# First expert gather taken apart, overflow loop in a branch, residual formed later: one change to a mixture-of-experts kernel

## The chip, the cores and the metric

One core of one Trainium2 chip runs the whole kernel as one program. The metric is device time in microseconds (us) of one execution, and the number before is the median of three runs. The profile comes from one further execution, whose own time is given beside its span. Engines are named as in the profile: PE (matrix products), PEld (weight loads of PE), DVE (vector), ACT (scalar), POOL (GpSimd), SP (sync, which here only issues loads). All the weights are float32 and are read from HBM once.

## The reference

One decoder layer over 256 tokens of width 2048. What matters here is the middle and the end of it: a router picks two of 16 experts for each token, and the experts' weights, 3 x 8 MB each, are by far most of the bytes.

```python
x = layer_norm(ALPHA * x + mix, ln1_g[i], ln1_b[i])
ffn = grouped_top2_moe(x, w_router, b_router, w_e_gate[i], w_e_up[i], w_e_down[i])
x = layer_norm(ALPHA * x + ffn, ln2_g[i], ln2_b[i])
x = x + jax.nn.sigmoid(x @ w_ple_gate[i]) * (p[i] @ w_ple_proj[i])

# grouped_top2_moe, for expert e and the rows xb that chose it
hid = jax.nn.silu(xb @ w_gate[e]) * (xb @ w_up[e])      # 2048 -> 1024, twice
y   = (hid @ w_down[e]) * src_w[:, None]                # 1024 -> 2048
```

## The kernel before

The program runs in stages, and each engine executes its instructions in the order in which the code writes them. The head (input projection, gated DeltaNet, pooling, output projection) ends with the first layer norm, whose standardised rows lie in `x1`, and with the router. Then come the 16 experts' gate and up products, expert by expert (the loop `for e in range(NE)`), then all down products, one chunk of output columns after the other (`CH`, five chunks of 512, 512, 512, 256 and 256 columns) with the last gate matrix between them, and a tail that normalises and writes.

**Pieces and slots.** Gate and up weights travel in pieces of 128 partitions x 1024 floats (4 KB per partition, 512 KB in all). Two neighbouring rows of a gate or up matrix lie as one run of 8 KB in HBM; a load of whole runs fills two pieces. A piece waits for its product in a slot: `ring` (5) and `ht` (3) hold two pieces each, `pre` (6) and `raw` (4) one piece each. That is 26 pieces. `begin` issues the next load into a free slot, on SP's queue; if a two-piece slot meets two halves of the same run it is one load of 8 KB runs, otherwise two loads of 4 KB runs. `freed` is called when PE has read a piece and starts the next load into that slot at once.

**Gather.** Experts are handled in pairs. A one-hot matrix `P` (DVE, L971) picks the rows of `x1` that chose the two experts, 64 places each. `gather` multiplies `P` by `x1` in four column blocks (L1000), brings each to SBUF (L1006), transposes it (L1012) and writes it to the tile `X` (L1019, or L1024 and L1026 for the first pair, where the norm's scale and bias are applied on the way). The first gather runs whole before the first product; the next one is run in steps between the products of the first expert of the pair before.

**Residual.** After the first gather DVE multiplies `x1` by the norm's scale and adds its bias in place (L1100, L1101), from four broadcast rows that ACT's queue had loaded, and ACT writes ALPHA times that to `r0` (L1102).

**Overflow.** If more than 64 tokens choose one expert, the rest goes through a loop with a trip count read from memory (`overflow`, L1114 to L1193). It stands before expert 2 (`OVER = 2`). In the profiled execution the count is zero. A loop is built from blocks: a jump that skips the body, a skip block in which each engine waits until its own work is done (for SP: all loads that it has issued), and an exit block in which each engine waits for all the others.

**Products.** A piece is used by two product instructions, one per expert half of the array (L1089), which the trace shows as four rows. `step()` and `estep()` advance the side jobs (evacuation, gather, hidden layer) by one step after each piece.

Of the kernel before, what the change touches and what calls it, by code (L numbers as in the profile page):

```python
# [10 lines left out]
F32 = mybir.dt.float32  # L11
# [10 lines left out]
NE = 16  # L22
# [8 lines left out]
RING, HTS, HLN, OVER = 5, 3, 8, 2  # L31
# [12 lines left out]
def trunk(tc, x, p, w_in, conv_w, a_log, dt_bias, dn_norm_w, pool_w, pool_scale, w_out,  # L44
# [4 lines left out]
    with es:  # L49
# [646 lines left out]
        SLOTS = {"ring": (RING, 2), "ht": (HTS, 2), "pre": (6, 1), "raw": (4, 1)}  # L696
# [6 lines left out]
        def slot_tile(tag, dtype=F32):  # L703
            bufs, n = SLOTS[tag]
            return spool[tag].tile([128, 1024 * n], dtype, name=tag, tag=tag, bufs=bufs)
# [91 lines left out]
        row4 = {}  # L797
# [31 lines left out]
        for cs, ks in wout_order[1:]:  # L829
            for c in cs:  # L830
# [13 lines left out]
        for tag in ("raw", "pre"):  # L844
            for _ in range(SLOTS[tag][0]):
                begin(tag)
# [77 lines left out]
        def choice():  # L924
# [5 lines left out]
            nc.vector.tensor_copy(ntoti, ntot)  # L930
            nc.vector.tensor_reduce(c2[1], pr, axis=AX.X, op=ALU.add)
# [25 lines left out]
        for _ in range(HTS):  # L957
            begin("ht")

# [32 lines left out]
        def gather(P, X, raw=False):  # L992
# [22 lines left out]
            def put(c, ps):  # L1015
                v = X[c // 2][:, c % 2 * 4:c % 2 * 4 + 4]
                ps = ps.rearrange("p (k s) -> p k s", s=128)
                if not raw:
                    (nc.vector.tensor_copy if c % 2 else nc.scalar.copy)(v, ps)  # L1019
                    return  # L1020
                for i in range(4):
                    g, b = (ln1p[:, i % 2, n, 2 * c + i // 2:2 * c + i // 2 + 1] for n in range(2))
                    if c % 2:
                        nc.vector.tensor_scalar(v[:, i], ps[:, i], g, b, op0=ALU.mult, op1=ALU.add)  # L1024
                    else:
                        nc.scalar.activation(v[:, i], ps[:, i], AF.Identity, bias=b, scale=g)  # L1026
# [87 lines left out]
        def overflow():  # L1114
            trips = nc.values_load(ntoti[0:1, 0:1], min_val=0, max_val=(2 * S - 1) // (SL + 1))
            with tc.For_i(0, trips, 1):  # L1116
# [30 lines left out]
                for c in range(2):  # L1147
                    ps = pt().rearrange("p (j s) -> p j s", s=SL)
                    for i in range(8):
                        d = c * 1024 + i // 2 * 256 + i % 2  # L1150
                        for t in range(NB):
                            nc.tensor.matmul(ps[:, i], x1[:, t, d:d + 256 - i % 2:2], Pv[:, t], start=(t == 0), stop=(t == NB - 1))
                    nc.scalar.copy(Xv[:, c * 8:c * 8 + 8], ps)
# [20 lines left out]
                nc.scalar.copy(Cv[SL:128], ps[0:SL, 0:S])  # L1174
                for c in range(4):
                    cs = slice(c * 512, (c + 1) * 512)
                    Y = pa()
                    for f0 in range(0, 8, 2):
                        src = wd[ds(e * DE + f0 * 128, 256), cs].rearrange("(k p) c -> p k c", p=128)
                        w = load(src, hl_tile("raw"))  # L1180
                        for i, v in enumerate(HALVES):
                            f = f0 + i
                            nc.tensor.matmul(Y[v], hv[0][:, f // 4, f % 4], w[:, i * 512:(i + 1) * 512], start=(f0 == 0), stop=(f0 == 6))
                    yy = hl_tile("yy", F32R).rearrange("p (n c) -> p n c", n=2)
                    nc.scalar.activation(yy[:, 0], Y, AF.Copy, scale=gv)
                    nc.vector.scalar_tensor_tensor(yy[:, 1], Y, gv, yy[:, 0], op0=ALU.mult, op1=ALU.subtract)
                    for t in range(NB):
# [3 lines left out]
                        nc.vector.tensor_add(r0[:, t, cs], r0[:, t, cs], ps)  # L1191
# [597 lines left out]
```

## Time and profile before

| what | value |
|---|---|
| median of 3 runs | 1578.21 us (1577.09 to 1580.15) |
| the profiled execution's own time | 1575.58 us |
| span of its instructions | 1573.7 us |
| PE busy | 1457.8 us, 93% of the span |
| DVE, ACT, POOL busy | 29%, 20%, 9% |
| bytes moved | 491.70 MB, mean 312 GB/s |

A stretch of the span is read in three steps: how busy the DMA engines are in it and how many GB/s they move, whether PE waits in it and for what, and what stands in the chain of work that ended last. A busy share of DMA of 1 or a little more means that the core's 16 DMA engines never pause.

### The profile page before, as it was taken

The numbers are of one execution on the slowest core, as the hardware profiler recorded it, in microseconds if no ns is written. First come the engines' busy times: TensorE is split into PE (matmuls) and PEld (weight loads), VectorE is DVE, ScalarE is ACT, GpSimd is POOL, SyncE is SP. The second block draws the span as 40 slices with busy tenths as digits, with TensorE's granted clock in tenths as the row PEclk, the third lists the DMA queues.
The fourth block names the chain that finished last, engine by engine and source line by source line (L and its number), as shares of the span: only waits on it lengthen the run. The fifth ranks groups of instructions, "written<-read, shape, count | busy, mean of one in ns | idle before, by whom it ended". The sixth has DMA issues, their size and how long they took to land.

```text
span 1573.7 us, 19926 instructions
## 1 busy us (share of the span) xinstructions
PE 1457.8 (93%) x8058; PEld 813.6 (52%) x8058; DVE 462.7 (29%) x866; ACT 313.5 (20%) x584; POOL 134.7 (9%) x210
## 2 busy tenths in 40 slices
PE   8999999999969759989889899988999999999997
PEld 8999989987833213322223232321233444546765
DVE  5885777665460000000001010000100101113335
ACT  4443443243331000000001010100010111002123
POOL 1251034310000000000000000000000000000023
PEclk9999999999999979999999999999999999999999
DMA  8544453448837969999999999999999999999991
GB/s 252 163 140 117 125 163 106 121 135 265 330 130 273 411 250 387 409 415 412 418 416 409 412 412 409 413 413 409 402 387 386 382 379 381 380 378 346 349 352 60
DMA packets 204387, 491.70 MB, mean 312 GB/s; under 512 B 18442, under 2 KB 64707, under 8 KB 193795
## 3 DMA queue, kind: packets, MB, share of 16 engines
q1 hardware_dynamic: 198784, 487.64, 83.8%
q10 hardware_dynamic: 5426, 2.48, 0.6%
q8 instruction: 65, 1.06, 0.3%
q14 instruction: 32, 0.25, 0.0%
q0 software_dynamic: 80, 0.26, 0.0%
HBM read 488.23 MB, written 2.10 MB: 312 GB/s over the span
## 4 chain that ended last, share of the span: by engine, by line
DMA 37%; PE 25%; DVE 1%; ACT 0%; issue 0%; POOL 0%; SPq 0%; ACTq 0%
PE pa L1640 9%; DMA ring<-in_w_e_up 7%; DMA ring<-in_w_e_gate 7%; DMA ht<-in_w_e_gate 5%; PE pa L1089 4%; PE pa L1558 4%; DMA ht<-in_w_e_up 4%; DMA ring<-in_w_e_down 3%; DMA ht<-in_w_e_down 3%; DMA pre<-in_w_e_gate 2%; DMA pre<-in_w_e_up 2%; PE pt L1000 2%; DMA ht<-in_w_ple_gate 2%; PE pt L1558 2%; PE pt L1456 2%; DMA pre<-in_w_e_down 1%
## 5 line engine op out<-in xcount | busy, mean ns | idle before, releaser
L1089 PE MATMUL pa<-ring,X 128*64 128x512 f32 x856 | 209.1, 606 | 21.2 <-DMA ring<-in_w_e_up 10.8
L658 PE MATMUL pp<-xh,hi 128*128 128x256 f32 x640 | 188.3, 294 | 0.0
L658 PE MATMUL pp<-xl,hi 128*128 128x256 f32 x640 | 179.7, 281 | 0.0
L658 PE MATMUL pp<-xh,lo 128*128 128x256 f32 x640 | 179.6, 281 | 0.0
L611 DVE TENSOR_TENSOR lo<-raw,hi 128x512 fp32r<-128x512 f32 x206 | 149.2, 748 | 90.3 <-ACT hi L610 90.0
L1089 PE MATMUL pa<-ht,X 128*64 128x512 f32 x648 | 159.3, 604 | 16.4 <-DMA ht<-in_w_e_gate 8.4
L610 ACT CAST hi<-raw 128x512 fp32r<-128x512 f32 x206 | 119.2, 618 | 140.1 <-PE pp L658 99.7
L1089 PE MATMUL pa<-pre,X 128*64 128x512 f32 x464 | 116.3, 607 | 30.7 <-SPq L1116 25.8
L1089 PEld LDWEIGHTS pa<-ring,X 128*64 128x64 f32 x856 | 52.8, 136 | 146.4 <-issue 66.9
L658 PEld LDWEIGHTS pp<-xh,hi 128*128 128x128 f32 x640 | 122.3, 191 | 0.2
L658 PEld LDWEIGHTS pp<-xl,hi 128*128 128x128 f32 x640 | 122.3, 191 | 0.1
L658 PEld LDWEIGHTS pp<-xh,lo 128*128 128x128 f32 x640 | 121.9, 190 | 0.1
L1078 DVE SCALAR_TENSOR_TENSOR evac<-evac,pt 128x512 f32<-128x512 f32 x16 | 11.0, 687 | 370.0 <-ACT evac L1075 370.0
L1089 PEld LDWEIGHTS pa<-ht,X 128*64 128x64 f32 x648 | 39.6, 136 | 113.2 <-issue 50.6
L1442 DVE SCALAR_TENSOR_TENSOR evac<-pa,gs,evac 128x512 fp32r<-128x512 f32 (+1 forms) x40 | 25.7, 642 | 190.0 <-ACT evac L1440 190.0
L1640 PE MATMUL pa<-ht,raw 128*64 128x512 f32 (+1 forms) x308 | 80.6, 511 | 0.7 <-DMA ht<-in_w_e_down 0.7
L1047 ACT COPY evac<-pa 128x512 f32<-128x512 f32 x32 | 18.8, 586 | 313.5 <-PE pa L1089 313.5
L1089 PEld LDWEIGHTS pa<-pre,X 128*64 128x64 f32 x464 | 28.7, 137 | 97.7 <-issue 61.3
L1640 PE MATMUL pa<-ring,pre 128*64 128x512 f32 (+1 forms) x296 | 78.0, 520 | 1.1 <-DMA ring<-in_w_e_down 1.1
L1000 PE MATMUL pt<-x,P 128*64 128x512 f32 x256 | 64.3, 627 | 12.6 <-DVE P L971 12.5
L1640 PE MATMUL pa<-ring,raw 128*64 128x512 f32 (+1 forms) x256 | 68.0, 514 | 1.1 <-DMA ring<-in_w_e_down 1.1
L1640 PE MATMUL pa<-ht,pre 128*64 128x512 f32 (+1 forms) x244 | 64.8, 517 | 1.0 <-DMA ht<-in_w_e_down 1.0
(377 smaller groups left out, 1807.0 us busy)
## 6 DMA issues: line engine op xcount, KB each, us to landing
ring<-in_w_e_down SPq DMA_DIRECT2D x111, 512.0 KB, 10.8
ht<-in_w_e_down SPq DMA_DIRECT2D x110, 512.0 KB, 10.5
raw<-in_w_in SPq DMA_DIRECT2D x80, 512.0 KB, 3.7
ring<-in_w_e_up SPq DMA_DIRECT2D x62, 512.0 KB, 10.2
pre<-in_w_e_gate SPq DMA_DIRECT2D x60, 512.0 KB, 10.2
ring<-in_w_e_gate SPq DMA_DIRECT2D x29, 1024.0 KB, 13.6
pre<-in_w_e_up SPq DMA_DIRECT2D x56, 512.0 KB, 10.2
ht<-in_w_e_gate SPq DMA_DIRECT2D x53, 512.0 KB, 10.2
```

The costliest lines, as they stand in the source:

```text
L610: nc.scalar.copy(hi[:, k], raw[:, k])
L611: nc.vector.tensor_sub(lo[:, k], raw[:, k], hi[:, k])
L658: nc.tensor.matmul(o, a[:, k, hc], b[:, kk], start=(first and n == 0), stop=(last and n == 2), skip_group_check=True)
L1000: nc.tensor.matmul(ps[v], P[:, t, a], x1[:, t, c * 512:(c + 1) * 512], start=(t == 0), stop=(t == NB - 1))
L1047: nc.scalar.copy(raw, acc)
L1078: nc.vector.scalar_tensor_tensor(h, h, 1.0, tr[0], op0=ALU.add, op1=ALU.mult)
L1089: nc.tensor.matmul(acc[v], X(kk), w[:, h * 512:(h + 1) * 512], start=(kk == 0), stop=(kk == KC - 1))
L1442: nc.vector.scalar_tensor_tensor(yy[1], Y, gs[:, e:e + 1], yy[0], op0=ALU.mult, op1=ALU.subtract)
L1456: nc.tensor.matmul(pR[c][t], C[:, e, t * 128:(t + 1) * 128], yy[n], start=(e == 0 and n == 0 and (t == 0 or w == 512)), stop=(e == NE // 2 ...
L1558: nc.tensor.matmul(ps[:, 0:S + 2], a[:, o:o + 128], b[:, k], start=(k == 0 and n == 0), stop=(k == kn - 1 and n == len(pairs) - 1))
L1640: nc.tensor.matmul(Y[v], HS[2 * e + a][:, f // 4, f % 4], two_[a][0][:, j * w:(j + 1) * w], start=(f == 0), stop=(f == 7))
```

## The change

It does six things. (1) The first gather is done without transposes: `gather0` multiplies a block of `x1` (as weights, with every second column) by `P` and gets `X` in its final layout; two of its four blocks run before the first product, the other two just before pieces 0 and 4 of expert 0. (2) Each later gather starts one expert later, with the second expert of the pair before. (3) `x1` is left standardised; every gather applies scale and bias on its way to `X`, and `r0` starts as zeros (POOL) and is filled by the new side job `residual`, from expert 1 on. The four broadcast rows are no longer loaded. (4) The overflow loop moves ahead of expert 0 and into a branch, `tc.If(trips > 0, ...)`. (5) `pre` has 8 slots instead of 6, the pool `hl` 6 tiles instead of 8, and two `X` tiles that are not yet needed are lent to the first loads ("X", `lent`). (6) Single slots are refilled two at a time, so that two-piece slots always meet whole 8 KB runs.

```diff
-RING, HTS, HLN, OVER = 5, 3, 8, 2
+RING, HTS, HLN = 5, 3, 6
...
-        SLOTS = {"ring": (RING, 2), "ht": (HTS, 2), "pre": (6, 1), "raw": (4, 1)}
+        SLOTS = {"ring": (RING, 2), "ht": (HTS, 2), "pre": (8, 1), "raw": (4, 1), "X": (4, 1)}
...
-                if c == 1:
-                    for n, v in (("g", ln1_g), ("b", ln1_b)):
-                        for h in range(2):
-                            row4[n, h] = hl_tile("row")
-                            nc.scalar.dma_start(row4[n, h], v[None, h * 1024:(h + 1) * 1024].to_broadcast([128, 1024]))
...
+        for _ in range(2):
+            begin("X")
+        nc.gpsimd.memset(r0, 0.0)
...
+        def gather0(P, X):
+
+            for c in range(4):
+                ps = pt().rearrange("p (k s) -> p k s", s=128)
+                for i in range(4):
+                    for t in range(NB):
+                        nc.tensor.matmul(ps[:, i], channels(t, 4 * c + i), P[:, t].rearrange("p n s -> p (n s)"),
+                                         start=(t == 0), stop=(t == NB - 1))
+                scaled_in(X[c // 2][:, c % 2 * 4:c % 2 * 4 + 4], ps, 4 * c, 4, nc.vector if c % 2 else nc.scalar)
+                ps = None
+                yield
...
+        beyond()
         Xs = [x_tiles()]
-        run(gather(P0, Xs[0], True))
-        choice()
-        for t in range(NB):
-            for h in range(2):
-                v = x1[:, t, h * 1024:(h + 1) * 1024]
-                nc.vector.tensor_tensor(v, v, row4["g", h], op=ALU.mult)
-                nc.vector.tensor_tensor(v, v, row4["b", h], op=ALU.add)
-                nc.scalar.mul(r0[:, t, h * 1024:(h + 1) * 1024], v, ALPHA)
-        row4 = None
+        first = gather0(P0, Xs[0])
+        for _ in range(2):
+            next(first)
...
+        def residual():
+
+            nc.vector.tensor_scalar(lna, lncol[:, 0:2], ALPHA, None, op0=ALU.mult)
+            for c in range(4):
+                cs = slice(c * 512, (c + 1) * 512)
+                for a in range(2):
+                    gc = hl_tile("gc")[:, 0:512].rearrange("p (k j) -> p k j", j=128)
+                    nc.gpsimd.tensor_copy(gc, lna[:, a, 4 * c:4 * c + 4, None].to_broadcast([128, 4, 128]))
+                    for _ in range(3):
+                        yield
+                    ps = pt()
+                    for k in range(4):
+                        nc.tensor.transpose(ps[:, k * 128:(k + 1) * 128], gc[:, k], ident)
+                    gc = None
+                    yield
+                    for t in range(NB):
+                        v = ps
+                        if a == 0:
+                            v = evac_tile()
+                            nc.vector.tensor_tensor(v, x1[:, t, cs], ps, op=ALU.mult)
+                        nc.vector.tensor_add(r0[:, t, cs], r0[:, t, cs], v)
+                        v = None
+                        yield
+                    ps = None
...
-            with tc.For_i(0, trips, 1):
+            with tc.If(trips > 0, preferred_fallthrough_block=False), tc.For_i(0, trips, 1):
...
+        spare = {1: deque(), 2: deque()}
+        owed = ["X"] * 2
+
+        def lend():
+            while todo:
+                if spare[2]:
+                    begin(spare[2].popleft())
+                elif len(spare[1]) > 1:
+                    for _ in range(2):
+                        begin(spare[1].popleft())
+                else:
+                    return
...
+        choice()
+        overflow()
         for _ in range(LOOKP):
             take()
...
-            if e == OVER:
-                while bg:
-                    step()
-                overflow()
+            if e == 1:
+                ends.append(residual())
...
-                if e + 2 < NE:
-                    P0 = onehot(pr + 1)
-                    Xs.append(x_tiles())
-                    bg.append(gather(P0, Xs[-1]))
+            elif e + 1 < NE:
+                P0 = onehot(pr + 1)
+                Xs.append(x_tiles())
+                bg.append(gather(P0, Xs[-1]))
...
+                    if e == m == 0 and kk in (0, 4):
+                        next(first)
```

On PE, at the start of expert 0, the order before is: the first gather whole, one piece's product, and then the second pair's gather between the next pieces (`pt` and `pa` are tiles in PSUM; ring and raw are the slots).

```order
L1000 MATMUL pt<-x_4283,P 64x512 x8
L1012 MATMUL pt<-ident,xg 128x128 x4
...
L1012 MATMUL pt<-ident,xg 128x128 x8
L1089 MATMUL pa<-ring,X 64x512 x2
L1000 MATMUL pt<-x_4283,P 64x512 x4
L1089 MATMUL pa<-ring,X 64x512 x2
L1000 MATMUL pt<-x_4283,P 64x512 x4
L1089 MATMUL pa<-ring,X 64x512 x2
L1012 MATMUL pt<-ident,xg 128x128 x4
```

After the change the same place reads as follows; the rows between the branches and the last group belong to the overflow's body, which is jumped over.

```order
L1013 MATMUL pt<-P,x_4283 128x128 x16
L1156 TENSOR_LOAD ntoti
L1157 COMPARE_AND_BRANCH
L1157 UNCONDITIONAL_BRANCH
...
L1013 MATMUL pt<-P,x_4283 128x128 x8
L1108 MATMUL pa<-ring,X 64x512 x8
L1013 MATMUL pt<-P,x_4283 128x128 x8
L1108 MATMUL pa<-ring,X 64x512 x12
L1108 MATMUL pa<-raw,X 64x512 x8
```

The branch has come ahead of the first product, the two later blocks of the first gather stand before pieces 0 and 4, and the second pair's gather (L1000 before, L1027 now) is gone from this place. On SP's queue the order before, from the last loads of the first filling to the loop, is this.

```order
L775 DMA ht<-in_w_e_up 128x2048 x3
L775 DMA ring<-in_w_e_up 128x2048 x3
L775 DMA ring<-in_w_e_gate 128x2048 x2
...
L775 DMA ring<-in_w_e_gate 128x2048 x2
L775 DMA ring<-in_w_e_up 128x2048 x3
L775 DMA raw<-in_w_e_up 128x1024 x3
L1115 TENSOR_LOAD ntoti
L1115 ISA x2
L1116 COMPARE_AND_BRANCH
```

After the change SP meets the branch with only the first filling behind it.

```order
L777 DMA pre<-in_w_e_up 128x1024 x6
L777 DMA ht<-in_w_e_up 128x2048 x3
L777 DMA lent<-in_w_e_up 128x1024 x2
L1156 TENSOR_LOAD ntoti
L1156 ISA x2
L1157 COMPARE_AND_BRANCH
...
L777 DMA ring<-in_w_e_up 128x2048
L777 DMA ring<-in_w_e_gate 128x2048 x4
L777 DMA raw<-in_w_e_gate 128x1024 x3
```

The loop was reached behind two experts' refills; the branch is reached before any refill. In the built program the false side of the branch holds, for each engine, a wait for its own work alone (on SP for all loads so far) and a jump over the body; the block in which every engine waits for all others is left on the true side only. Over the whole queue the loads of gate and up weights with whole 8 KB runs (128x2048) go from 82 to 174.

## Rows read from the trace of the kernel before

**Rows 1.** Stretches of the span; columns: length, busy (instructions) of each engine, clock, DMA share, GB/s.
```profile
core 0: us, PE busy (x) PEld busy (x) DVE busy (x) ACT busy (x) POOL busy (x), PEclk, DMA share, GB/s
449.50:477.67 28.17, 15.44 (x64) 5.42 (x62) 15.90 (x32) 8.99 (x15) 0.00 (x0) 0.77 0.00 1
477.67:500.00 22.33, 22.33 (x106) 7.66 (x104) 2.77 (x4) 2.34 (x4) 0.00 (x0) 0.99 0.77 270
500.00:548.00 48.00, 42.68 (x200) 14.22 (x196) 2.75 (x4) 2.94 (x5) 0.00 (x0) 0.99 1.03 411
548.00:605.00 57.00, 36.44 (x160) 12.35 (x162) 3.35 (x6) 2.93 (x5) 0.00 (x0) 0.77 0.76 285
605.00:1124.00 519.00, 474.90 (x2088) 141.29 (x2084) 41.17 (x71) 44.90 (x78) 1.52 (x4) 1.00 1.02 412
...
1236.00:1420.00 184.00, 183.60 (x788) 88.21 (x790) 21.75 (x38) 17.18 (x34) 0.00 (x0) 1.00 1.05 379
1420.00:1533.50 113.50, 109.57 (x866) 79.19 (x864) 42.00 (x78) 27.13 (x39) 13.17 (x14) 1.00 1.08 350
```
**Rows 2.** PE's timeline at the first products: start, length, what, idle before and releaser.
```profile
448.70 3.65 PE L1000 MATMUL pt<-x,P 128*64 128x512 f32 x16
452.28 0.66 PE L1012 MATMUL pt<-ident,xg 128*128 128x128 f32 x4
452.87 1.94 PE L1000 MATMUL pt<-x,P 128*64 128x512 f32 x8
...
458.64 1.08 PE L1089 MATMUL pa<-ring,X 128*64 128x512 f32 x4
472.24 3.68 PE L1000 MATMUL pt<-x,P 128*64 128x512 f32 x8 [12.52 <-DVE P L971]
...
477.41 2.34 PE L1000 MATMUL pt<-x,P 128*64 128x512 f32 x8
```
**Rows 3.** Timelines of SP and DVE around the first products.
```profile
439.88 0.57 SPq L775 DMA_DIRECT2D ht<-in_w_e_up  x1
477.67 0.33 SPq L775 DMA_DIRECT2D ring<-in_w_e_up  x1
...
462.32 1.22 DVE L1100 TENSOR_TENSOR x<-x,row 128x1024 f32<-128x1024 f32 x1
...
471.90 0.49 DVE L971 TENSOR_TENSOR P<-slot,posx 128x128 f32<-128x128 f32 x2
```
**Rows 4.** Loop lines L1116, L1115: durations ns minimum/median/maximum, first and last start.
```profile
L1116 SPq EVENT_SEMAPHORE  x2: 17/17/17, 552.8 to 563.8; - x2
...
L1116 PEldq COMPARE_BRANCH  x3: 101/197/5952, 542.8 to 568.3; - x3
...
L1115 PEldq TENSOR_LOAD <-ntoti x1: 487/487/487, 542.1 to 542.1; - x1
```
**Rows 5.** Timelines of PE and SP after the overflow loop.
```profile
568.56 1.98 PE L1089 MATMUL pa<-pre,X 128*64 128x512 f32 x4 [25.78 <-SPq L1116]
...
571.04 12.52 SPq L775 DMA_DIRECT2D pre<-in_w_e_up  x6
```
**Rows 6.** Chain of work that ended last, pieces in order of time.
```profile
602.13 10.16 DMA ring<-in_w_e_gate
...
1225.39 10.97 DMA ring<-in_w_e_down
...
1421.77 9.01 DMA ht<-in_w_ple_gate
```
**Rows 7.** Line L611, durations as in rows 4.
```profile
L611 DVE TENSOR_TENSOR lo<-raw,hi x206: 630/689/2386, 7.6 to 425.3; 128x512 fp32r<-128x512 f32 x103
```
**Rows 8.** POOL's timeline late in the span, a memset.
```profile
1530.83 1.84 POOL L1579 MEMSET pre<- 68x1024 f32 x2
```
**Rows 9.** DMA totals of 645 to 665, then of 765 to 785.
```profile
DMA packets 2251, 8.19 MB, mean 410 GB/s; under 512 B 251, under 2 KB 251, under 8 KB 2251
...
DMA packets 1355, 8.41 MB, mean 421 GB/s; under 512 B 150, under 2 KB 150, under 8 KB 506
```

More of the change, by code (lines that the diff above doesn't have):

```diff
@@ L704, in slot_tile @@
             bufs, n = SLOTS[tag]
+            if tag == "X":
+                return keep_tile("lent", dtype)[:, 0:1024]
             return spool[tag].tile([128, 1024 * n], dtype, name=tag, tag=tag, bufs=bufs)
@@ L838, in trunk @@
                 xr = None
-                if c == 1:
-                    for n, v in (("g", ln1_g), ("b", ln1_b)):
-                        for h in range(2):
-                            row4[n, h] = hl_tile("row")
-                            nc.scalar.dma_start(row4[n, h], v[None, h * 1024:(h + 1) * 1024].to_broadcast([128, 1024]))
-        for tag in ("raw", "pre"):
-            for _ in range(SLOTS[tag][0]):
+        for tag, n in (("raw", 4), ("pre", 8)):
+            for _ in range(n):
                 begin(tag)
@@ L930, in choice @@
             nc.vector.tensor_copy(ntoti, ntot)
+        def choice():
             nc.vector.tensor_reduce(c2[1], pr, axis=AX.X, op=ALU.add)
@@ L990, in trunk, with scaled_in, channels, gather @@
         HALVES = (slice(0, SL), slice(SL, 128))
-        def gather(P, X, raw=False):
+        def scaled_in(v, ps, k, n, eng):
+            for i in range(n):
+                g, b = (ln1p[:, (k + i) % 2, a, (k + i) // 2:(k + i) // 2 + 1] for a in range(2))
+                if eng is nc.vector:
+                    nc.vector.tensor_scalar(v[:, i], ps[:, i], g, b, op0=ALU.mult, op1=ALU.add)
+                else:
+                    nc.scalar.activation(v[:, i], ps[:, i], AF.Identity, bias=b, scale=g)
+        def channels(t, k):
+            d = k // 2 * 256 + k % 2
+            return x1[:, t, d:d + 256 - k % 2:2]
+        def gather0(P, X):
[8 more added lines that the diff above has]
+                yield
+        def gather(P, X):
             xg = [hl_tile("xg") for _ in range(2)]
@@ L1017, in put @@
                 ps = ps.rearrange("p (k s) -> p k s", s=128)
[L1018 to L1026, printed above, removed]
+                scaled_in(v, ps, 4 * c, 4, nc.vector if c % 2 else nc.scalar)
             was, now = pick(0), None
@@ L1149, in overflow @@
                     for i in range(8):
-                        d = c * 1024 + i // 2 * 256 + i % 2
                         for t in range(NB):
-                            nc.tensor.matmul(ps[:, i], x1[:, t, d:d + 256 - i % 2:2], Pv[:, t], start=(t == 0), stop=(t == NB - 1))
-                    nc.scalar.copy(Xv[:, c * 8:c * 8 + 8], ps)
+                            nc.tensor.matmul(ps[:, i], channels(t, 8 * c + i), Pv[:, t], start=(t == 0), stop=(t == NB - 1))
+                    scaled_in(Xv[:, c * 8:c * 8 + 8], ps, 8 * c, 8, nc.scalar)
                 ps = pt()
@@ L1174, in overflow @@
                 nc.scalar.copy(Cv[SL:128], ps[0:SL, 0:S])
+                misc = tri = Pv = ps = None
                 for c in range(4):
@@ L1191, in overflow @@
                         nc.vector.tensor_add(r0[:, t, cs], r0[:, t, cs], ps)
+                        ps = None
+                    Y = yy = None
                 nc.vector.tensor_scalar(icnt, icnt, 1.0, None, op0=ALU.add)
-                misc = tri = Pv = Xv = raws = hv = acc = Cv = Y = yy = ps = None
+                raws = hv = Cv = None
         def cols_src(w, r0_, rn, c0, cn):
@@ L1254, in freed @@
             else:
-                spare.append(slot_[0])
-                while todo and spare:
-                    begin(spare.popleft())
+                spare[SLOTS[slot_[0]][1]].append(slot_[0])
+                lend()
         held = {k: deque() for k in ("hold", "keep")}
```

12 lines of the change are left out of this document (6 added, 6 removed).

## The prediction

> **What bounds the kernel now.** I began with the table of stretches [rows 1], because it shows in one view when the weights flow. Three things are to be seen. From 449.5 to 477.67 the DMA engines stand still (share 0.00): every slot is full and nothing has been used up. From 500 on their share is 1.02 to 1.08 in every stretch shown but one, up to 1533.5: they never pause, and the rate hangs only on what is loaded (412 GB/s for gate and up, 379 and 350 later, where shorter runs are loaded). The exception is 548 to 605 with 0.76. From 1533.5 to the span's end at 1573.7 a tail follows without weights. So after 477.67 the span is the time of the remaining bytes, plus what the DMA engines lose in two holes, plus the tail. PE is 93% busy in the page's sum, but that does not make it the bound of the experts' stage: there it has 44 us free of 519.
>
> Next the timelines of both holes. The first: PE gathers from 448.70, does one piece at 458.64, and then stands 12.52 us before the second gather's first product at 472.24, released by DVE's `P` [rows 2]. DVE has by then worked eight instructions of 1.22 us on `x1` (462.32 to 471.9) before it comes to that `P`. The first refill is issued at 477.67, when the second piece has been read [rows 3]; the last load of the first filling was issued at 439.88. The second: SP enters the loop's skip block at 552.8 and comes out of its last wait at 563.8 [rows 4], since there it waits for all its loads. The next product starts at 568.56 after 25.78 us of idle PE, the next refill is issued at 571.04 [rows 5], and refills then go at the pace at which PE frees slots between the gather's products.
>
> Last the chain [rows 6]: from 602 to 1236 it is loads nearly throughout, then PE until 1421.77, while the DMA share stays above 1. In the down stage both are close to their limit.
>
> **The first start.** What does the new order make of the 477.67? `P` is there when PE starts at 448.70. A block of `gather0` is 16 rows in the trace's way of counting (8 products in float32). The nearest row is the transpose with 128 columns and a full weight load, L1012: four of them in 0.59 us until the next starts (452.28 to 452.87), 0.147 each [rows 2], so 2.35 us a block. Lower bound: L1000 moves 512 columns, two half arrays at a time, at 3.58/16 = 0.224 each (448.70 to 452.28); a quarter of twice that is 0.112, or 1.8 us a block. Upper bound: the 0.66 that the view gives the four, 2.65 us.
>
> Two blocks: 453.4. POOL now clears `r0` (128 x 4096) at about 441 to 445, while DVE computes the routing. Whether DVE is held by that no row shows; DVE's longest L611 took 2.386 us against a median of 0.689 [rows 7], so something can hold it. Two memsets of 1024 took POOL 1.84 us [rows 8], so this one takes about 3.7, and that is the most it can cost. Between the ends I take 1.0: 454.4. The Trainium skill ("SBUF — State Buffer", Who interferes with whom) says that a DVE copy or tensor_scalar in a two-port mode is blocked for the whole of a GpSimd instruction, and a tensor_tensor only by one that reads SBUF; by it nearly the whole memset could stand in front of the routing's tensor_scalar instructions, some 3 us later than without.
>
> Then the branch. Before the loop PE started to read the count at 542.1 and took the first branch at 542.8; with the wait behind it I count 1.0. Of its three branches the longest, the jump over the body, took 5.952 us, the others 0.101 and 0.197 [rows 4]. Before, it was hidden under SP's wait; now it is in front of the first product. It happened with all DMA engines busy, and now it meets a filling that is about to end. Between 0.1 and 5.95 I take 3.0: 458.4. The Trainium skill ("Runtime: NRT & Kernel Launch", Instruction fetch mechanics) has instructions streamed in order, and a taken branch out of the loaded window waits for a DMA. The trace's 5.952 agrees with a miss, the short jumps of the same line with hits. By that rule the price is all or nothing, which shifts the sum by 3 us either way.
>
> Third block 2.35: 460.8. Two pieces of four rows like L1000's, 0.9 us each, and 0.3 to the issue (477.41 to 477.67): the first refill at 462.8, that is **14.9 us earlier** (bounds 8 and 20). SP is through by then: its false side waits only for the first filling, and DMA fell idle at 449.5 before the change.
>
> **The deeper filling.** 30 pieces instead of 26 come in before the start; four more are 2.10 MB, at 411 GB/s **5.1 us** (0 to 5.1). With them the filling ends near 454.6, ahead of 462.8.
>
> **The slow refill after the start.** From 477.67 to 500 the rate was 270 against 411 [rows 1]: 22.33 x (1 - 270/411) = 7.7 us lost, mostly because the second gather stood between the pieces. It now comes an expert later, and PE, at 0.9 us a piece against 1.28 for the DMA engines (0.524 MB at 411), frees slots faster than they fill: in expert 0's 30 us it frees 16.8 MB and 12 MB come in. I leave 2.5 us for the first latency: **5.2 us** (0 to 7.7).
>
> **The loop.** From 548 to 605 the rate was 285: 57 x (1 - 285/411) = **17.5 us** (7 to 17.5; the low end if only the empty 564 to 571 goes). After the change nothing stands there: no wait of all engines for all, and no gather on a drained queue.
>
> **Whole runs.** 92 loads of 1.05 MB change from 4 KB to 8 KB runs, 96.5 MB. A stretch with none of the long runs moved 410 GB/s, one with mostly long ones 421 [rows 9]: 235.4 - 229.2 = **6.2 us** (0 to 7.5).
>
> **What is added, and where it hides.** `residual` gives PE 8 x 0.59, DVE 24 x about 0.69 (L611's median) and POOL eight copies, spread over some 56 pieces. DVE is busy 41 us of 519 there and PE has 44 free, so it costs nothing while the DMA engines are the bound; without that cover PE's 4.7 us. Four small instructions per block in place of one at `X` lie on the same idle DVE and ACT. The four broadcast rows leave ACT's queue, at a time when nobody waits for it. Two `hl` tiles fewer can make ACT and DVE wait before they split a gate piece in the last two chunks (12 such pieces, each two of L611's width, 1.4 us on DVE: 17 us in all); they are split two pieces ahead, so I take 1 us (0 to 17).
>
> Sum: 14.9 + 5.1 + 5.2 + 17.5 + 6.2 - 1.0 = 47.9 us. The profiled execution took 1575.58, so it would be 1527.7; the median of the runs lies 2.6 above it: **1530 us**.
>
> **Rivals.** (a) *The down stage gives it back.* PE bounds 1236 to 1421 and the chunks behind it alternate between PE and loads [rows 6], and the `hl` tiles are fewer. Against it: PE's start in that stage moves with the loads, and no PE work is added there. If all 17 us of splits show, the time is 1546. (b) *The branch holds the start.* If the jumps stall every engine one after the other and PE comes to its second piece no earlier than now, the first and third terms go: 17.5 + 5.1 + 6.2 - 1.0 = 27.8, hence 1550. For it speaks the 5.952, against it that 15 us must be lost. (c) *Slower: single slots held back.* A freed single slot now waits for a second one before both are loaded. 97 pairs of gate and up loads go that way in the queue's new order; if each leaves the DMA engines idle for one piece (1.28 us), that is 124 us and the time 1654. It turns the sign from 48 of them, 39%, on. Against it: in a stage that waits for loads the free slots are already issued, 10 us of loads deep (10.16 in the chain), so a lone slot is not missed. (d) *The branch does not do what it says*, and a wait of all for all stays where it was: then the loop's 17.5 and most of the start are not won, 1565 to 1578.
>
> **How the numbers follow.** The forecast has 0.74 (its own range 1520 to 1540, from the bounds of the start, the refill and the runs together), (a) 0.12, (b) 0.08, (c) 0.04, (d) 0.02. To leave out at most 2 in 10, the range goes from 1519 into (a): 1519 to 1547. A difference under 0.2% (3 us) can't be told from none here. Faster has 0.94, same 0.02 (part of d), slower 0.04 (c).
>
> **What would show it.** The DMA share should be 0 for some 8 us instead of 28 before the first product, and stay at 1 from about 465 to about 1484, with no hole near 540 and no idle PE of 25 us. The first product should come near 461, with one long branch row on PE ahead of it. The rate from 605 on should be near 416, not 412. I would be wrong if the DMA share in the experts' stage fell below 1 while PE waits (c), if PE's branch row were far over 6 us (b), or if PE waited for ACT or DVE at the last two chunks' gate products (a).

## The result, and the profile after

The changed kernel took 1536.01 us (median of 4 runs, 1535.27 to 1537.05), the kernel before 1577.65 (1576.58 to 1580.15) beside it: a ratio of 0.9734, 95% interval 0.9717 to 0.9751. The profiled execution took 1537.05 us with a span of 1534.7, 39.0 less than before. The forecast was 1530 in a range of 1519 to 1547, and the difference lies mostly in one place, the start. The first view is the table of stretches of the changed kernel; the columns are those of [rows 1].

```profile
core 0: us, PE busy (x) PEld busy (x) DVE busy (x) ACT busy (x) POOL busy (x), PEclk, DMA share, GB/s
...
452.90:470.84 17.94, 11.67 (x59) 9.04 (x60) 2.98 (x14) 3.01 (x8) 0.00 (x0) 0.74 0.02 5
470.84:500.00 29.16, 29.16 (x144) 10.87 (x142) 1.86 (x7) 1.17 (x2) 2.27 (x4) 1.00 0.92 359
500.00:548.00 48.00, 46.32 (x224) 16.18 (x220) 17.18 (x30) 5.83 (x13) 2.45 (x4) 1.00 1.01 414
548.00:605.00 57.00, 57.00 (x270) 19.46 (x268) 9.76 (x18) 7.02 (x15) 0.00 (x0) 1.00 1.02 415
605.00:1085.00 480.00, 438.57 (x1976) 138.39 (x1974) 47.89 (x103) 52.06 (x105) 1.52 (x4) 1.00 1.02 417
1197.00:1381.00 184.00, 184.00 (x791) 88.12 (x790) 21.99 (x38) 17.18 (x34) 0.00 (x0) 1.00 1.05 378
1381.00:1494.00 113.00, 109.29 (x858) 78.70 (x856) 41.89 (x78) 27.24 (x39) 13.84 (x14) 0.98 1.09 349
```

The hole of 548 to 605 [rows 1] is gone: share 1.02 and 415 GB/s, with PE busy throughout. The experts' stage runs at 417 GB/s instead of 412. The two stages behind it have the rates that they had (378 and 349), and loads end near 1494 as against 1533.5. The start is the exception: the empty stretch is still 18 us long where 8 were expected, and PEclk in it is 0.74. PE's timeline of the changed kernel shows what holds the first refill back.

```profile
449.26 0.58 PE L911 MATMUL pm<-M,cols 128*128 128x16 f32 x2 [3.58 <-DVE M L909]
449.68 0.59 PE L912 MATMUL pm<-M,cols 128*128 128x16 f32 x2
...
453.54 4.91 PE L1013 MATMUL pt<-P,x 128*128 128x128 f32 x32
462.24 0.63 PE L1013 MATMUL pt<-P,x 128*128 128x128 f32 x2 [3.78 <-DVEq L1157]
465.26 3.35 PE L1013 MATMUL pt<-P,x 128*128 128x128 f32 x14 [2.39 <-issue]
468.54 3.97 PE L1108 MATMUL pa<-ring,X 128*64 128x512 f32 x16
472.44 2.15 PE L1013 MATMUL pt<-P,x 128*128 128x128 f32 x16
```

Three stops stand there: 3.58 us in front of the routing's product L911, 3.78 at the branch, and 2.39, two rows behind the branch, for which the timeline names no releaser (the last section says what stands beside it). The third block (rows 462.24 and 465.26) takes 6.30 us with its stop; the same work at 472.44, at the upper clock level, takes 2.15. DVE, POOL and SP in the same stretch, each from its own timeline, say what the first stop waits for and when the first refill goes:

```profile
441.06 3.51 POOL L960 MEMSET r<- 128x4096 f32 x1
```
```profile
441.62 3.00 DVE L882 TENSOR_SCALAR c<-rs 128x2 f32<-128x2 f32 x1
...
461.06 0.19 DVE L936 TENSOR_TENSOR gate<-w,c 128x32 f32<-128x32 f32 x1
```
```profile
470.84 0.34 SPq L777 DMA_DIRECT2D ring<-in_w_e_up  x1
```

A DVE instruction on 128 x 2 elements takes 3.00 us and ends when POOL's clearing of `r0` ends. The same instruction took 0.16 us in the kernel before. The branch's own rows (durations in ns: minimum, median, maximum; first and last start) give PE's jump:

```profile
L1157 PEldq COMPARE_BRANCH  x2: 95/1760/3424, 456.8 to 458.6; - x2
...
L1157 DVEq COMPARE_BRANCH  x2: 51/53/55, 461.7 to 461.9; - x2
```

PE's long jump runs from 458.6 to 462.0, and DVE's last branch row starts at 461.9, so both are through at about the same time.

The chain of waits that ended last now begins its long part with PE's own pieces; from 604 to 1196 it is mostly loads, as before [rows 6], then PE, and near the end PE and loads by turns:

```profile
558.96 19.89 PE pa L1108 x92
...
604.64 16.49 DMA ring<-in_w_e_gate
...
1185.05 10.84 DMA ring<-in_w_e_down
...
1454.92 9.49 DMA ring<-in_w_ple_gate
```

### The profile page after: what moved, and what is told of

It is laid out like the page before. It is cut to its first block, busy times and chain, and to the rows that moved or that the text cites. A ratio compares the mean times of both kernels' runs of the same rounds, so it can differ in the third digit from the quotient of the medians.

```text
span 1534.7 us, 20076 instructions
## 1 busy us (share of the span) xinstructions
PE 1451.1 (95%) x8106; PEld 829.3 (54%) x8106; DVE 479.4 (31%) x923; ACT 320.5 (21%) x620; POOL 139.9 (9%) x219
## 4 chain that ended last, share of the span: by engine, by line
PE 34%; DMA 29%; DVE 1%; ACT 1%; issue 0%; POOL 0%; SPq 0%; ACTq 0%
PE pa L1108 11%; PE pa L1696 10%; DMA ring<-in_w_e_up 5%; DMA ring<-in_w_e_gate 5%; DMA ring<-in_w_e_down 4%; PE pa L1614 4%; DMA ht<-in_w_e_up 4%; DMA ht<-in_w_e_down 4%; DMA pre<-in_w_e_gate 3%; PE pt L1027 2%; PE pt L1614 2%; PE pt L1512 2%; DMA pre<-in_w_e_up 1%; DMA ring<-in_w_ple_proj 1%; DMA pre<-in_w_ple_proj 1%; DMA ht<-in_w_e_gate 1%
## 5 line engine op out<-in xcount | busy, mean ns | idle before, releaser
L1108 PE MATMUL pa<-ring,X 128*64 128x512 f32 x792 | 188.6, 602 | 15.2 <-DMA ring<-in_w_e_up 10.7
L611 DVE TENSOR_TENSOR lo<-raw,hi 128x512 fp32r<-128x512 f32 x206 | 148.0, 742 | 92.3 <-ACT hi L610 91.9
L1108 PE MATMUL pa<-ht,X 128*64 128x512 f32 x600 | 146.1, 603 | 20.6 <-DMA ht<-in_w_e_gate 11.7
L1108 PE MATMUL pa<-pre,X 128*64 128x512 f32 x576 | 137.6, 599 | 3.4 <-DMA pre<-in_w_e_gate 2.0
L1108 PEld LDWEIGHTS pa<-pre,X 128*64 128x64 f32 x576 | 37.6, 136 | 85.0 <-issue 58.1
L1496 ACT ACTIVATE evac<-pa,gs 128x512 fp32r<-128x512 f32 (+1 forms) x40 | 24.0, 600 | 191.3 <-PE pa L1696 180.5
L1696 PE MATMUL pa<-ht,raw 128*64 128x512 f32 (+1 forms) x252 | 60.9, 511 | 0.5 <-DMA ht<-in_w_e_down 0.5
L1696 PE MATMUL pa<-ring,raw 128*64 128x512 f32 (+1 forms) x224 | 55.7, 525 | 1.5 <-DMA ring<-in_w_e_down 1.4
L1696 PE MATMUL pa<-ring,pre 128*64 128x512 f32 (+1 forms) x236 | 55.3, 516 | 1.0 <-DMA ring<-in_w_e_down 1.0
```

What stands on the lines that cost most here:

```text
L611: nc.vector.tensor_sub(lo[:, k], raw[:, k], hi[:, k])
L1108: nc.tensor.matmul(acc[v], X(kk), w[:, h * 512:(h + 1) * 512], start=(kk == 0), stop=(kk == KC - 1))
L1496: nc.scalar.activation(yy[0], Y, AF.Copy, scale=gs[:, e:e + 1])
L1696: nc.tensor.matmul(Y[v], HS[2 * e + a][:, f // 4, f % 4], two_[a][0][:, j * w:(j + 1) * w], start=(f == 0), stop=(f == 7))
```

## The experiments

The theory under test is the prediction's: the end follows what the DMA engines get done, so each empty microsecond of theirs counts one to one, wherever it stands. Its rival is that later stages take a gain of the start up. Times are medians; the changed kernel's is 1536.01, and the kernel before took 1577.39, 1577.72, 1574.86 and 1577.29 beside the four groups of runs (e1 to e4, e5 to e8, e11, e12 to e14). The ratio compares a run with the kernel before of its own group and is estimated from all their executions, so it is not quite the quotient of the medians.

| run | us | range | ratio to before, interval |
|---|---|---|---|
| e1, DVE clears r0 | 1530.41 | 1529.5 to 1532.67 | 0.9705, 0.9689 to 0.9721 |
| e2, no overflow | 1528.26 | 1527.22 to 1533.48 | 0.9705, 0.9682 to 0.9728 |
| e3, before without the loop | 1560.07 | 1559.36 to 1562.29 | 0.9898, 0.9881 to 0.9915 |
| e4, before with the branch | 1571.88 | 1569.27 to 1572.85 | 0.9966, 0.9951 to 0.998 |
| e5, old refill rule | 1538.17 | 1537.16 to 1539.1 | 0.9755, 0.9739 to 0.9771 |
| e6, loop without branch | 1535.38 | 1534.14 to 1536.64 | 0.9735, 0.9719 to 0.9751 |
| e7, 26 pieces | 1541.92 | 1537.97 to 1542.3 | 0.977, 0.9751 to 0.9789 |
| e8, e7 with early gather | 1546.51 | 1543.63 to 1547.29 | 0.9808, 0.9791 to 0.9824 |
| e11, e1 with body inline | 1528.98 | 1526.62 to 1529.84 | 0.9708, 0.9692 to 0.9724 |
| e12, six pieces first | 1532.47 | 1530.85 to 1533.02 | 0.9715, 0.9699 to 0.9731 |
| e13, eight pieces first | 1533.13 | 1531.19 to 1535.07 | 0.9718, 0.9702 to 0.9734 |
| e14, e12 with body inline | 1528.3 | 1524.45 to 1530.08 | 0.969, 0.9671 to 0.9709 |

**e1: the clearing moved to DVE.**

```diff
-        nc.gpsimd.memset(r0, 0.0)
...
         beyond()
+        nc.vector.memset(r0, 0.0)
```

> The changed kernel, but r0 is cleared by DVE just after the small instructions of beyond(), where DVE waits 5.1 us for PE, and no longer by POOL beside the routing. Theory (the end follows the first refill one to one): L882 takes about 0.17 us instead of 3.00, PE does not stop 3.58 us in front of L911 and keeps the upper clock level, the gather starts near 448.9 instead of 453.54 and the first refill is issued near 465 instead of 470.84; the time falls by 5 to 6 us, to about 1530.5. Rival 1 (the start no longer sets the end, the later stages take the gain up): the first refill moves the same way, the time stays within 0.2% of 1536. Rival 2 (POOL was not what held L882): L882 still takes about 3 us and nothing moves.

Timelines of DVE, PE and SP in this run:

```profile
441.64 0.16 DVE L882 TENSOR_SCALAR c<-rs 128x2 f32<-128x2 f32 x1
...
450.42 3.47 DVE L1113 MEMSET r<- 128x4096 f32 x1 [0.80 <-issue]
```
```profile
446.50 0.37 PE L911 MATMUL pm<-M,cols 128*128 128x16 f32 x2 [0.81 <-DVE M L909]
...
448.82 5.54 PE L1012 MATMUL pt<-P,x 128*128 128x128 f32 x32
```
```profile
467.18 0.34 SPq L777 DMA_DIRECT2D ring<-in_w_e_up  x1
```

POOL's instruction was what held L882, so rival 2 falls. The first refill was expected near 465 and came at 467.18, 3.7 us earlier than in the changed kernel. The median fell by 5.6, the spans of the two profiled executions differ by 4.3 (1534.7 and 1530.4), and the loads up to 500 account for that: by the tables of stretches (440 to 450, to 470, to 500) e1 moved 382, 74 and 394 GB/s against 378, 49 and 349, 1.9 MB more, 4.5 us of loads. No run of e1 was as slow as the fastest of the changed kernel. Rival 1 falls. PE's second stop stayed (2.33 us). That PE "keeps the upper clock level" did not hold, and this is the part of the refill that was missed: two blocks took 5.54 us at a granted clock of 0.69 (448.80 to 454.30), against 4.01 at 1.00 in e11. PE's stop ahead of them was 0.81 us here and 0.80 in e11, so why the clock fell in one and not in the other stays open.

**e2: the changed kernel without the overflow path** (the call is left out; it has no trips here).

```diff
         choice()
-        overflow()
```

> The changed kernel without the overflow path (branch and loop left out; it has no trips in this input). Theory: PE goes from the second block of gather0 to the third without the 4.0 us of the jump and without the second stop of 2.4 us behind it; with the part of the third block's time that the lower clock takes (3.35 us for 14 rows against 2.15 for 16) the first refill comes 6.4 to 7.8 us earlier, near 463.8, and the time falls by as much, to about 1529. Rival 1 (the later stages take it up): within 0.2% of 1536. Rival 2 (the stop behind the jump has another cause than the branch, a wait for DVE or a late tile): only about 4 us go.

The three blocks of `gather0` now run in one piece, 7.35 us from 453.75, the first refill comes at 463.00, 7.8 us earlier, and the median falls by 7.7 us. The four runs lie 6 us apart, so the time alone is weak evidence against rival 2, which would have given 4; PE's timeline decides, since without the branch the second stop is gone too. So it belongs to the branch. The clearing is still on POOL here, so e1's gain is not in it.

**e3 and e4: the kernel before, without the loop, and with the loop inside the branch at its old place.** (e3 leaves the overflow path out.)

```diff
                 while bg:
                     step()
-                overflow()
```

> The kernel before without the overflow loop (left out; it has no trips in this input), everything else as before. Theory: the hole from 548 to 605 goes whole, 17.5 us, and the time falls from 1577.6 to about 1560 (1558 to 1562). Rival (the loop's wait is partly given back in later stages, and the 39 us of the change come from elsewhere): 7 us or less.

```diff
-            with tc.For_i(0, trips, 1):
+            with tc.If(trips > 0, preferred_fallthrough_block=False), tc.For_i(0, trips, 1):
```

> The kernel before with the overflow loop inside a branch, at its old place before expert 2. Theory: the other engines no longer wait for SP; SP alone still waits for all its loads, so DMA pauses only from the last landing (about 563) to the first new load (2 to 3 us) and then has many free slots; 12 to 15 us of the 17.5 are won, time about 1564. Rival (the place decides: any branch in the running stage empties the queue, PE stands as long): less than 5 us won, time 1573 or more.

e3 took 17.3 us less, the hole's price within a microsecond (412 GB/s from 548 to 605). e4 won only 5.5, close to the rival's number. Its table of stretches, the branch's rows and PE's timeline:

```profile
548.00:605.00 57.00, 43.76 (x186) 15.02 (x188) 2.77 (x4) 3.52 (x6) 0.00 (x0) 0.82 0.87 329
```
```profile
L1116 SPq EVENT_SEMAPHORE  x9: 17/17/17, 553.5 to 568.7; - x9
...
L1116 PEldq COMPARE_BRANCH  x2: 95/3145/6195, 543.7 to 544.0; - x2
```
```profile
550.43 1.97 PE L1089 MATMUL pa<-pre,X 128*64 128x512 f32 x4 [6.71 <-DMA ht<-in_w_e_gate]
...
569.40 1.12 PE L1012 MATMUL pt<-ident,xg 128*128 128x128 f32 x4 [10.81 <-ACT xg L1006]
```

The branch does free PE from the wait of all for all: it goes on at 550.43. But SP still waits for all its loads, until 568.7, and ACT's `xg` of the gather is held until then; the waits on L1116 show ACT and DVE idle for 25.2 and 22.4 us behind it. The price by the rates is 57 x (1 - 329/412) = 11.5 us, against 17.5 before: 6.0 of difference, 5.5 measured. The theory's "the other engines no longer wait for SP" was wrong, and so was its last landing "about 563". It agrees with the prediction's "last wait at 563.8", which was read from a view that ends at 564 [rows 4]. In the kernel before SP waits on in the skip block, as the same line shows from 567 to 568:

```profile
L1116 SPq EVENT_SEMAPHORE  x5: 17/17/17, 567.6 to 567.9; - x5
```

So the branch at the old place let SP go no earlier. Of the rival's reason the emptied queue was right; that PE stands as long was not (6.71 and 10.81 us instead of 25.78). That the end follows the DMA engines held.

**e5: the old refill rule on the changed kernel.**

```diff
-            while todo:
-                if spare[2]:
-                    begin(spare[2].popleft())
-                elif len(spare[1]) > 1:
...
+            while todo and spare:
+                begin(spare.popleft())
```

> The changed kernel with the refill rule of before: one queue of free slots, each refilled at once, so that many two-piece slots meet two halves of different runs and load 4 KB runs. Theory: the rate from 605 to 1085 falls from 417 to about 412 GB/s, as it was before, and the time rises by 5 to 6 us to about 1541.5. Rival 1 (the rate does not hang on the length of the runs, it came with the other parts): no change, 1536. Rival 2 (holding single slots back costs something that the longer runs only cover): less than 3 us slower, or faster.

2.2 us slower, with ranges that just do not overlap: too small to be told well by the times. The stretch shows it:

```profile
605.00:1085.00 480.00, 441.01 (x1960) 138.51 (x1957) 46.44 (x99) 52.11 (x105) 1.51 (x4) 0.99 1.02 414
```

414 GB/s instead of 417 is 480 x 3/417 = 3.5 us. The expectation forgot that the old rule depends on where the slots lie in the queue: with eight `pre` slots it still makes 120 loads of whole runs, against 174 in the changed kernel and 82 before. So 54 of the 92 were undone, for which the prediction's price is 6.2 x 54/92 = 3.6 us. The rate speaks against rival 1; rival 2, less than 3 us, is not excluded by the time.

**e6: the loop at its new place without the branch.**

```diff
-            with tc.If(trips > 0, preferred_fallthrough_block=False), tc.For_i(0, trips, 1):
+            with tc.For_i(0, trips, 1):
```

> The changed kernel with the overflow loop at its new place, but with no branch around it, so that its exit block makes all engines wait for each other and for SP's loads. Theory (the place counts: the first filling has landed by 453, before PE gets there): SP is through before PE, PE waits for DVE's side of the loop at most, 0 to 3 us slower, 1536 to 1539. Rival (the branch counts: the wait of all for all costs wherever it stands): 10 us or more slower, first refill at 480 or later.

No difference: first refill at 470.50, PE's long jump 3.341 us. Where the first filling has landed before PE arrives, the wait of all for all has no load to wait for. The 17.5 us were won by the place: the new place does it without the branch, and the branch at the old place won 5.5.

**e7 and e8: 26 pieces, and in e8 the later gathers one expert earlier.**

```diff
-        for tag, n in (("raw", 4), ("pre", 8)):
+        for tag, n in (("raw", 4), ("pre", 6)):
...
-        for _ in range(2):
-            begin("X")
...
-        owed = ["X"] * 2
+        owed = []
...
-            elif e + 1 < NE:
+                if e + 2 < NE:
...
```

> The changed kernel with the old depth of the first filling: 6 pre slots instead of 8 and no X tiles lent, 26 pieces instead of 30. Theory: DMA goes idle 5.1 us earlier and starts again when it does now, so the time rises by 5 us, to about 1541. Rival (later slots make it up, or 30 pieces never mattered since PE in the down stage sets the end): less than 2 us.

> As the run with 26 pieces, and in addition the later gathers one expert earlier, as they were before: the gather for experts 2 and 3 stands between the first products of expert 0 (the lent X tiles would be in its way, hence 26 pieces). Theory: PE frees slots at a slower pace just after the start, the rate to 500 falls from about 359 to near 290 GB/s, 3 to 5 us more than the run with 26 pieces alone, about 1545. Rival (the gather is hidden under the loads wherever it stands): no more than 1 us from the run with 26 pieces.

Both as the theory had it: 5.9 us for the four pieces, 4.6 more for the early gather. From 470 to 500, first e7 and then e8, in their tables of stretches:

```profile
470.00:500.00 30.00, 30.00 (x146) 11.19 (x147) 1.86 (x7) 2.09 (x5) 2.27 (x4) 0.98 0.87 335
```
```profile
470.00:500.00 30.00, 30.00 (x150) 11.51 (x148) 5.57 (x15) 4.69 (x11) 3.39 (x6) 1.00 0.74 270
```

PE is busy for all 30 us in both; in e8 its work is the gather instead of pieces, and 65 GB/s x 30 us / 412 GB/s = 4.7 us of loads are missing.

**e11: e1 with the branch laid out the other way round.**

```diff
-            with tc.If(trips > 0, preferred_fallthrough_block=False), tc.For_i(0, trips, 1):
+            with tc.If(trips > 0, preferred_fallthrough_block=True), tc.For_i(0, trips, 1):
```

> The run with DVE's clearing (1530.4), with the branch laid out the other way round: the overflow body stands directly behind the compare, and the side that is taken here stands behind the body, next to the code that follows. Theory (both stops of PE are code that is brought in after PE leaves the straight line): one long jump either way, PE stands about 3.6 us and again about 2.3 us, time 1530 within 1.5. Rival (the second stop belongs to the second jump of the old layout): it goes, 2.3 us less, about 1528.

The times don't tell it from e1. In PE's timeline the stops are 4.39 and 0.63 us:

```profile
448.52 4.01 PE L1012 MATMUL pt<-P,x 128*128 128x128 f32 x32
456.91 0.68 PE L1012 MATMUL pt<-P,x 128*128 128x128 f32 x2 [4.39 <-DVEq L1157]
458.21 2.78 PE L1012 MATMUL pt<-P,x 128*128 128x128 f32 x14 [0.63 <-issue]
```

PE's jump (3.852 us from 450.9) is over at 454.8, and PE stands until DVE, which has cleared `r0` and worked off `choice`, leaves the branch at 456.7. So DVE's part of the branch is a wait of its own. That `choice` behind the branch would take it away was not tried.

**e12, e13, e14: loads into the dead time.** Built on e1; six or eight pieces of expert 0 come before the branch, and in e14 the branch of e12 has e11's layout. (The loop's body, which has no trips here, keeps its sums in the `pt` tiles. In e9 and e10, the same two orders with these sums left in `pa`, the program deadlocks, and neither has a time.)

```diff
         choice()
-        overflow()
...
                 for kk in range(KC):
-                    if e == m == 0 and kk in (0, 4):
+                    if e == m == 0 and kk == 6:
+                        overflow()
+                    if e == m == 0 and kk in (8, 10):
                         next(first)
```

> The run with DVE's clearing (1530.4), and the overflow branch moved from in front of expert 0 to behind its first six pieces (the body of the loop, which has no trips here, keeps its sums in other PSUM tiles); the third and fourth block of gather0 come before pieces 8 and 10. Theory (the end follows what the DMA engines get done in the empty time): the first refill is issued near 456.5, three loads of 1.05 MB (7.7 us at 411 GB/s) flow while PE stands 6 us in the jump and behind it, the next refill comes near 468.3 instead of 467.18; gain 7.7 - 1.1 = 6.6 us, time about 1524. Rival (SP's wait for its own loads in the branch now reaches past PE's stop, and what follows waits for SP, as in the run with the branch at its old place, where PE stood 10.81 us): gain of 0 to 3 us, 1527.5 or more.

> As the run with six pieces ahead of the branch, but eight: four loads of 1.05 MB (10.2 us) flow during the stop, but PE reaches the branch 1.8 us later and must do the third block of gather0 right behind it, so that the next refill comes near 472.3. Theory: gain over 1530.4 of 10.2 - 5.1 = 5 us, about 1525.5, a little behind the run with six. Rival (SP's wait for its loads decides): it is slower than with six by the 2.6 us by which the last load lands later, and at 1529 or more.

> The run with six pieces ahead of the branch, with the branch laid out the other way round (the overflow body directly behind the compare, the side that is taken here behind the body). In the profile of the run with that layout and the branch in front of expert 0, the second stop was 0.63 us instead of 2.3, but its median (1529.0) could not be told from 1530.4. Theory (the second stop belongs to the layout): 1.7 us shorter stop than in the run with six pieces, time 1 to 2 us less. Rival (the shorter stop was chance of that one execution): same time within 1 us, second stop near 2.3 again.

In e12 the first refill was issued at 456.96, and nothing was won: SP left its wait at 468.8, 2 us after PE was back, and the hole of the DMA engines stood from 464 to 472 (129 GB/s) instead of ahead of 467. The rival was right in that SP's wait reaches past PE's stop and that nothing is won, but PE itself stood for its jump and not for SP. e13 went the same way, 0.7 us slower than e12 and not the rival's 2.6. Part of it is the jump, which now happens while loads flow. The branch's rows of e12, then of e14:

```profile
L1157 SPq EVENT_SEMAPHORE  x9: 17/17/17, 461.7 to 468.8; - x9
...
L1157 PEldq COMPARE_BRANCH  x2: 95/3090/6084, 457.2 to 460.6; - x2
...
L1157 PEldq EVENT_SEMAPHORE  x1: 51/51/51, 460.4 to 460.4; - x1
```
```profile
L1157 SPq EVENT_SEMAPHORE  x9: 17/17/17, 464.0 to 466.5; - x9
...
L1157 PEldq COMPARE_BRANCH  x1: 5592/5592/5592, 454.2 to 454.2; - x1
...
L1157 PEldq EVENT_SEMAPHORE  x1: 51/51/51, 459.9 to 459.9; - x1
```

And PE's restart, e12 first:

```profile
466.80 3.47 PE L1107 MATMUL pa<-ring,X 128*64 128x512 f32 x8 [6.45 <-issue]
```
```profile
451.99 5.37 PE L1107 MATMUL pa<-ring,X 128*64 128x512 f32 x24
460.15 3.59 PE L1107 MATMUL pa<-ring,X 128*64 128x512 f32 x8 [2.79 <-PEq L1157]
```

In e12 PE compares at 457.2, waits until its own products are done (460.4), and only then takes the long jump, with nothing left to do. In e14 the long jump is the compare itself, taken at 454.2 while products still run until 457.36, and the wait comes behind it. PE stands 2.79 us instead of 6.45, and the time is 4.2 us less, with ranges apart. Neither reason of the expectation fits: there is no second stop in e12 or in e14, and what the layout changed is the cover of the jump. e14 has the lowest ratio of the versions that keep the overflow path, 0.969, and its interval lies below that of the changed kernel (up to 0.9709, against 0.9717 and more); it overlaps those of e1 and e11, so it is not shown to be faster than they are.

## Why the prediction was right, and where its terms were off

The direction and the mechanism held: each experiment that moved the DMA engines' empty time moved the end by about as much, and no gain was given back behind 605. The bytes say the same. On the weights' queue q1 (packets, MB, share) the profiled executions before and after had moved this much by 1085 us:

```profile
q1 hardware_dynamic: 91875, 316.74, 77.4%
```
```profile
q1 hardware_dynamic: 83247, 333.34, 79.8%
```

The 16.6 MB are 40.0 us at 415 GB/s, and the spans differ by 39.0. Counted in this way against the changed kernel, the profiled executions of the experiments come within 1.3 us of their spans, except e2, e8 and e11 (2.3 to 3.0).

Rivals (a) and (c) were not seen: the rates from 1085 on are the old ones, and the DMA share did not fall. In the stretch from 1381 to 1494 PE waited for neither ACT nor DVE at the splits, so the 1 us for the `hl` tiles was not paid (no run undid that edit alone). Rival (d) failed by the missing hole, and in e6 a wait of all for all at the new place cost nothing. Rival (b) was nearer: the start gained less than half of what was forecast, though PE's second piece did come earlier, and half of the loss was not the branch's. That `residual` costs nothing was not tested by a run of its own; PE had 41 us free of 480 in that stage. Nor was the new gather undone by itself.

| term | predicted | from the profile after | run |
|---|---|---|---|
| first refill earlier | 14.9 | 477.67 - 470.84 = 6.8 | e1, e2 |
| deeper filling | 5.1 | filling ends near 452.9, not 449.5 | e7: 5.9 |
| slow refill after the start | 5.2 | 7.7 - 29.16 x (1 - 359/415) = 3.8 | e8 - e7: 4.6 |
| the loop | 17.5 | 548 to 605 at 415 | e3: 17.3 |
| whole runs | 6.2 | 480 x 5/417 = 5.8 | e5: 2.2 for 54 of 92 loads |
| `hl` tiles | -1.0 | 0 | - |
| sum | 47.9 | 39.0 (the spans; medians 41.6) | |

The term that was mis-sized is the first start: the refill was put at 462.8 and came at 470.84, 8.0 later, which leaves a gain of 6.8, below the term's lower bound of 8. Of the 8.0, 3.8 come ahead of the first block and 3.95 in the third block. By the prediction's steps:

- **"Between the ends I take 1.0" for POOL's memset.** It cost 4.8 (PE's `gather0` began at 453.54, after 448.70 before): 2.8 by L882, near the upper end of 3.7, and the rest by the clock, which was at the lower of its two levels (1.2 GHz; granted 0.50 from 449.26 to 451.38) when PE went on after its stop, so that L911 to L915 came 0.42 apart instead of 0.22. The Trainium skill ("SBUF — State Buffer", Who interferes with whom) has a tensor_scalar in a two-port mode blocked for the whole of a GpSimd instruction; 3.00 us of L882, which ends with the MEMSET of 3.51, agree with it. That L882 ran in such a mode is not shown by any run. e1 shows that the memset was the cause.
- **The branch, 4.0 with the reading.** PE stood 3.78 (458.46 to 462.24). That the sum fits is luck: the reading cost nothing, since it ran beside the second block's products (456.2), and the jump took 3.42 instead of 3.0, a value that was only chosen between two ends.
- **"Third block 2.35".** It took 6.3. 2.39 of that is the second stop, for which the prediction had no term at all; e2 shows that it goes with the branch. The other 1.6 us are the lower clock level (14 rows in 3.35 us, at 0.50).
- **Two blocks and two pieces** were right within about 0.2 us. For the blocks that is luck in part: two took 4.91 at a granted clock of 0.79, and 4.01 at 1.00 (e11).
- **"Last wait at 563.8"** is a misreading (see e4); only the lower end of the loop's bounds hung on it.

That the branch mattered only by its place (e6) was not the prediction's wording: it named the missing "wait of all engines for all" as the reason. At the old place the branch alone is worth 5.5 us (e4).

## What to carry to other kernels

When the loads never pause, look for the stretches where they do, and price a change by the empty time of the DMA engines that it removes; in e1 to e8, where the empty time was known, that price held within 2 us. What missed was the forecast of when the first refill would go out. A wait of one queue for all its own loads costs little only where those loads have landed already, so place a loop or branch there, and let the long jump run while products are still queued (e14 against e12, 4.2 us). Before moving a memset to an idle engine, look at what small instructions of another engine run beside it on the critical path.

## What the runs showed of the hardware

PE's long jump was never short, and its length went with the state of the DMA engines: 3.424, 3.341, 3.644, 3.664 and 3.852 us where they had run dry or were about to (changed kernel, e6, e1, e5, e11), and 5.952, 6.195, 6.084, 6.144 and 5.592 while loads flowed (before, e4, e12, e13, e14). The Trainium skill ("Runtime: NRT & Kernel Launch", Instruction fetch mechanics) has a taken branch out of the loaded window wait for a DMA. The trace agrees: beside the weights' queue it shows queues of the kind "instruction", and in each of these ten jumps one load of 16 KB starts on the queue q8. Here are the changed kernel from 458.6 to 462.1, then e12 from 460.5 to 466.7 (packets, MB, share):

```profile
q8 instruction: 1, 0.02, 1.9%
```
```profile
q8 instruction: 1, 0.02, 1.0%
```

It starts 1.0 to 1.2 us after the jump in the first five and 3.2 to 3.8 us after it in the others, takes 1.0 to 1.4 us, and the jump ends 1.3 to 1.5 us after the load is through. So what makes the jump longer while loads flow is the time until this load starts.

After the jump PE stopped a second time, 2.39, 2.33 and 2.30 us in the changed kernel, e1 and e5, but 0.63 in e11, 0.76 in e6, where PE had already waited for another engine behind its jump, and not at all in e12 to e14. By its timing this is the next load of code: in these five runs another 16 KB load starts on q8 0.7 us after the jump's end, and PE goes on 1.3 to 1.6 us after that load is through. In e2, without the branch, q8 has no load from 446 to 470, and there is no such stop. In e12 that load starts 0.8 us after the jump, and PE has eight rows to do meanwhile (3.47 us). The layout does not decide it: e12 has that of the changed kernel. Why the first load does not bring enough in some runs is not shown.
